# Early loading of the first MLP weights, and turnings without a tie to exponentials, in a two-layer decoder trunk

## The chip, the core and the metric

The kernel runs on one core of one Trainium2 chip. A core has a matrix engine (TensorE, called PE), a vector engine (VectorE, DVE), a scalar engine (ScalarE, ACT), a general engine (GpSimd, POOL) and a queue engine (SyncE, SP) that only issues DMA transfers here. Each engine works through its own list of instructions in order and waits on semaphores for the others. The metric is the device time of one execution in microseconds (us). The time before is 996.58 us, the median of three runs (995.73 to 997.40).

## What is computed

One sequence of 512 tokens of width 1024 goes through two layers, in float32. Layer A is latent attention with 8 heads (a compressed key and value of rank 256, a rotary part of 64), layer B is attention in a sliding window of 128 tokens with 16 query heads over 4 key heads, with a bias by distance and a sink for each head. Each mixer is followed by a LayerNorm and an MLP of width 4096, and the MLP by another LayerNorm:

```python
for l in range(2):
    if l == 0:
        y = _mla(x, ...)                      # softmax(q k') over c_kv, then w_uv, then o @ w_o
    else:
        k_band, v_band = _shared_kv(x, w_kv)  # bands of 2 * 128 tokens
        y = _swa(x, w_q, sinks, w_o, k_band, v_band, rel_bias)
    x = _layernorm(alpha * x + y, ln_mix_g[l], ln_mix_b[l])
    h = jax.nn.relu(x @ w_up[l])
    x = _layernorm(alpha * x + (h * h) @ w_down[l], ln_mlp_g[l], ln_mlp_b[l])
```

## The kernel before

**High and low parts.** A float32 product is made of three products of a shorter float type: every operand is split into a high part and the rest, and `three` (L106) gives the pairs high-high, high-low and low-high, which `group` (L103) sends to PE one after the other into one PSUM bank. `split` (L75) makes the parts: ACT copies the source into the short type (L77), and then DVE, in some cases POOL, subtracts the copy from the source (L81). So each weight tile takes a transfer, an ACT copy and a subtraction before PE can use it: the raw tile is `raw` or `wq`, the high part `wh`, the low part `wl`. The same function splits attention probabilities that have been turned (`pt`, in layer B `pth` and `ptl`) and heads' outputs (`oh`, `ol`).

**Order.** A scheduler orders the instructions on ACT, DVE and POOL by its own estimate of their times. The order of PE's instructions and of the SP transfers is that of the program text, through `pe` (L86). `behind` (L91) adds an edge: what is made inside is issued after the given instructions. `state["plain"]` holds the two instructions of the last split of an ordinary weight piece, `state["exp"]` the last exponential of layer B.

**The weight stream.** `queue` (L128) and `queue_seven` (L167) put weight pieces into the list `stream`, and `weights` (L314) prepares them four ahead of use, in the order of use. The raw tiles of ordinary pieces have two buffers, so a transfer waits until the subtraction of the piece two before has read its tile. The pieces of w_o are numbered 0 to 7 here. An MLP (width 4096 in four quarters) is computed with seven block products in place of eight, and `queue_seven` streams the blocks for one matrix and quarter. Its first pieces, `loaded` with block (0, 0) of the up matrix of quarter 0, fill a tile `wq` in two halves by two SP transfers of 512 KB (L210); their parts go into tiles set aside, w_fac and w_quada (`aside_of`, L157). `grown` ties those two splits behind the last ordinary split (L190), which is one of w_o.

**Layer A's attention** runs in `run_steps` (L542) over 32 units (h, i), head by query block of 128. Each unit computes scores (L1130) three units ahead of the turning (L1172), and a head's products with the values (`mix`, L1188) come two units behind. The scores end in a maximum on DVE (L1160), an exponential on ACT (L1165), a reciprocal (L1168) and a product (L1169) on DVE. Other work is put between the units from the list `fill`, whose entries have a cost, a unit by which they are due, a unit before which they don't come, and a function. The last entries load x's four token tiles (`load_x_tokens`, L925) and compute parts of the projection with w_o (`proj.part`). Then `proj.finish` (L501) makes the rest: the left halves of the four token tiles, then the right halves with, for each tile, the residual add (L584), the statistics, and `layer_norm` (L436, with its last steps at L446 and L449). The normed tile is turned on PE by eight transposes (L688) for the MLP.

**Layer B's attention** runs in the same way over 16 heads. `scores` (L1319) makes for one head the sums with the bias and the maxima (L1342), the negative maximum `nb` (L1346) and four exponentials (L1350) from two score banks. `turn` (L1362) transposes the probabilities in two halves (L1370, L1372) and splits each (`pth` on ACT, `ptl` on DVE). The first half is behind the last exponential, the one of the head two ahead (L1375). `mix` (L1385) multiplies by the values and adds two halves into `o` (L1402).

## Time and profile before

| What | us |
|---|---|
| median of three runs | 996.58 (995.73 to 997.40) |
| profiled execution | 997.49 |
| its span, first to last instruction | 995.7 |
| PE busy | 984.8 (99%) |
| DVE busy | 772.4 (78%) |
| ACT busy | 555.3 (56%) |
| POOL busy | 214.4 (22%) |

The granted clock of TensorE was 0.999 of full speed. Times in the text are counted from the start of the span. A row of the timeline has the start, the duration, the engine, the line, the operation with its output and input tiles and shapes, the number of instructions in the row and, in brackets, how long the engine had been idle before it and for whom it had waited. Matmuls overlap, so a matmul starts before the one ahead of it has ended. A row of the waits has the engine and line that waited, whom for, the us in total, the times and the longest. A row of the windows has the stretch, its length and each engine's busy time with its count of instructions, the granted clock, the busy share of the DMA engines and GB/s. A row of the DMA issues ends with the KB of one transfer and the us from issue to landing.

### The profile page before, as it was taken

How to read it: one execution, taken by the hardware profiler on the slowest of the kernel's cores; microseconds unless marked ns; L12 is line 12 of the kernel's file. 1: busy time of each engine (PE TensorE's matmuls, PEld its weight loads, DVE VectorE, ACT ScalarE, POOL GpSimd, SP SyncE). 2: the span in 40 equal slices, each digit the busy share in tenths (PEclk: the TensorE clock that was granted, in tenths of full speed). 3: DMA queues.
4: the chain of work that ended last, by engine and by line, in shares of the span. 5: the costliest groups of instructions: out<-in, count | busy, mean ns of one | idle time of the engine just before them, and what ended most of it. 6: DMA issues, size and time to landing. Idle time of an engine off the chain costs nothing.

```text
span 995.7 us, 15827 instructions
## 1 busy us (share of the span) xinstructions
PE 984.8 (99%) x6103; PEld 888.2 (89%) x6103; DVE 772.4 (78%) x1242; ACT 555.3 (56%) x850; POOL 214.4 (22%) x203
## 2 busy tenths in 40 slices
PE   9999999999999999999999999999999999999997
PEld 9888888998999999998898998889998999999986
DVE  6589857989778769786686778698985986898756
ACT  5556644467547547646145798546763663664620
POOL 1231001121212212210002775112131122023000
PEclk9999999999999999999999999999999999999999
DMA  7431227489889977964232212359798798798422
GB/s 261 142 90 43 68 103 226 103 184 226 152 183 238 171 170 218 224 109 145 67 106 96 86 65 75 110 144 211 181 203 183 176 207 175 167 261 143 115 95 85
DMA packets 60678, 149.55 MB, mean 150 GB/s; under 512 B 5259, under 2 KB 10300, under 8 KB 60604
## 3 DMA queue, kind: packets, MB, share of 16 engines
q0 software_dynamic: 24320, 58.73, 33.2%
q1 hardware_dynamic: 36140, 89.56, 27.0%
q8 instruction: 48, 0.79, 0.3%
q10 hardware_dynamic: 144, 0.26, 0.1%
q14 instruction: 26, 0.21, 0.1%
HBM read 146.41 MB, written 4.22 MB: 151 GB/s over the span
## 4 chain that ended last, share of the span: by engine, by line
PE 95%; DVE 2%; DMA 1%; ACT 1%; issue 0%; SPq 0%; DVEq 0%; POOL 0%; POOLq 0%
PE mm L105 87%; PE tr L105 5%; DMA wq<-in_up 1%; PE tr L1181 1%; PE tr L688 1%; PE tr L1370 1%; PE tr L1372 0%; ACT wh L77 0%; PE tr L461 0%; DVE mm L1342 0%; DVE x L446 0%; DVE wl L81 0%; DVE x L449 0%; PE tr L949 0%; DVE ptl L81 0%
## 5 line engine op out<-in xcount | busy, mean ns | idle before, releaser
L105 PE MATMUL mm<-wh,fac 128*128 128x512 f32 (+1 forms) x944 | 292.6, 386 | 0.0
L77 ACT ACTIVATE wh<-wq 128x1024 fp32r<-128x1024 f32 x164 | 173.8, 1061 | 185.0 <-PE mm L105 133.7
L81 DVE TENSOR_TENSOR wl<-wq,wh 128x1024 fp32r<-128x1024 f32 x164 | 199.4, 1220 | 68.1 <-ACT wh L77 66.6
L105 PE MATMUL mm<-xth,wh 128*128 128x256 f32 (+1 forms) x928 | 243.4, 290 | 0.0
L105 PE MATMUL mm<-xth,wl 128*128 128x256 f32 (+1 forms) x800 | 233.2, 292 | 0.0
L105 PEld LDWEIGHTS mm<-wh,fac 128*128 128x128 f32 x944 | 176.2, 188 | 35.6 <-DVE fac L81 0.6
L105 PE MATMUL mm<-xtl,wh 128*128 128x256 f32 (+1 forms) x672 | 197.1, 293 | 0.0
L105 PE MATMUL mm<-wl,fac 128*128 128x512 f32 (+1 forms) x472 | 182.3, 386 | 0.0
L105 PEld LDWEIGHTS mm<-xth,wh 128*128 128x128 f32 x928 | 168.6, 192 | 3.2
L105 PEld LDWEIGHTS mm<-xth,wl 128*128 128x128 f32 x800 | 153.2, 192 | 2.6
L77 ACT ACTIVATE wh<-raw 128x1024 fp32r<-128x1024 f32 (+3 forms) x86 | 85.1, 990 | 99.6 <-PE mm L105 56.9
L105 PEld LDWEIGHTS mm<-xtl,wh 128*128 128x128 f32 x672 | 128.7, 192 | 3.0
L201 POOL DMA_DIRECT2D wq<-in_up x64 | 77.5, 1237 | 202.0 <-DVE wl L81 192.1
L81 DVE TENSOR_TENSOR wl<-raw,wh 128x1024 fp32r<-128x1024 f32 (+2 forms) x66 | 77.0, 1173 | 35.8 <-ACT wh L77 35.5
L105 PEld LDWEIGHTS mm<-wl,fac 128*128 128x128 f32 x472 | 88.8, 188 | 16.5
L201 POOL DMA_DIRECT2D wq<-in_down x48 | 42.0, 875 | 187.2 <-DVE wl L81 181.3
L81 POOL TENSOR_TENSOR wl<-raw,wh 128x1024 fp32r<-128x1024 f32 (+2 forms) x20 | 41.3, 2067 | 87.5 <-ACT wh L77 82.0
L419 POOL TENSOR_TENSOR rs<-mv,half 128x1 f32<-128x1 f32 x16 | 8.8, 553 | 226.1 <-DVE mv L440 226.1
L105 PE MATMUL mm<-wh,oh 128*128 128x512 f32 x128 | 50.9, 398 | 0.0
L105 PE MATMUL mm<-wh,ol 128*128 128x512 f32 x128 | 50.1, 391 | 0.0
L105 PE MATMUL mm<-wl,oh 128*128 128x512 f32 x128 | 50.0, 390 | 0.0
L587 DVE TENSOR_TENSOR x<-mm,x 128x512 f32<-128x512 f32 (+1 forms) x49 | 32.9, 674 | 15.8 <-PE mm L105 15.7
(222 smaller groups left out, 1817.7 us busy)
## 6 DMA issues: line engine op xcount, KB each, us to landing
wq<-in_up POOLq DMA_DIRECT2D x64, 512.0 KB, 8.4
wq<-in_down POOLq DMA_DIRECT2D x48, 512.0 KB, 7.2
wq<-in_up SPq DMA_DIRECT2D x32, 512.0 KB, 6.8
raw<-in_down SPq DMA_DIRECT2D x28, 512.0 KB, 6.7
wq<-in_down SPq DMA_DIRECT2D x24, 512.0 KB, 5.9
raw<-in_up SPq DMA_DIRECT2D x16, 512.0 KB, 3.9
raw<-in_w_o SPq DMA_DIRECT2D x8, 512.0 KB, 5.1
raw<-in_w_sq SPq DMA_DIRECT2D x8, 512.0 KB, 3.3
```

The costliest lines, as they stand in the source:

```text
L77: high = nc.scalar.activation(dst_h, src, AF.Copy)
L81: low = (engine or nc.vector).tensor_sub(dst_l, src, f32(dst_h))
L105: pe(nc.tensor.matmul(dst, st, mv, start=first and i == 0, stop=last and i == len(pairs) - 1, **kw))
L201: nc.gpsimd.dma_start(half(a, jp), chunk(*more, jp), accum_op=ALU.add)
L419: state["rs"] = nc.gpsimd.tensor_tensor(r, v, half, ALU.pow)
L587: nc.vector.tensor_add(xs[t][:, c], b, xs[t][:, c])
L688: pe(nc.tensor.transpose(pt[:, a, :], xs[t][:, k * P : (k + 1) * P], ident))
L1181: pe(nc.tensor.transpose(pt[:, kb * P : (kb + 1) * P], p[:, kb * P : (kb + 1) * P], ident))
L1370: pe(nc.tensor.transpose(pt[:, a, 0:P], p[:, kb, P:256], ident))
```

## The change

The change has two parts.

In the first, the two SP transfers of layer A's first up block (the `wq` halves) become a function `preload`, which is put into `fill` right behind `load_x_tokens` and not before unit 17. So they are issued behind x's four tiles and ahead of w_o's piece 3, where before they came behind piece 7. `loaded` then issues no transfer for them, and `grown` no longer puts their splits behind the last ordinary split. Layer B's MLP calls no preload, and its code acts as before. On ACT and DVE the splits of w_fac and w_quada now stand ahead of those of w_o's pieces 4 and 5, behind the output of the last head; the split of piece 3 stands some places later than before, on ACT behind an exponential of head 7 and a turned block of head 6, on DVE behind a reciprocal, a small subtraction and a product.

In the second, `turn` of layer B ties the first half's split to `state["exp"]` only for heads 0 to 9. The order on the engines changes for the splits of heads 11 and 12 only: head 11's first half now stands ahead of its second half and of head 13's exponentials, and head 12's two halves stand ahead of head 14's exponentials. The sum `o` of head 10 now stands ahead of head 14's `nb`. The orders on PE and POOL are the same as before.

```diff
-        stream, off_ring, later = [], [], []
+        stream, off_ring, later, preloads = [], [], [], {}
...
+            early = set()
+
             def grown(a, jp, *more, aside=None):
                 wh, wl = tiles_of_weights(aside)
                 after = None
-                if aside:
+                if aside and not early:
                     after = state.pop("plain", None)
...
+            def preload():
+                for jp in range(2):
+                    early.add(jp)
+                    pe(nc.sync.dma_start(half("a", jp), chunk(0, 0, jp)))
+
+            preloads.setdefault((name, key), preload)
+
             def loaded(a, jp, at, *more, aside=None):
-                pe(nc.sync.dma_start(half(a, jp), chunk(*at, jp)))
+                if a == "b" or jp not in early:
+                    pe(nc.sync.dma_start(half(a, jp), chunk(*at, jp)))
                 return grown(a, jp, *more, aside=aside)
...
             fill.append((0, 99, -9, load_x_tokens))
+            fill.append((0, 99, 17, preloads["up", "U"]))
             for t in range(2):
                 for kp in range(3):
                     fill.append((1.3, 99, max(8 * kp + 10, 29 * t), lambda t=t, kp=kp: proj.part(t, kp)))
...
-                        with behind((state["exp"],)):
+                        with behind((state["exp"],) if h < 10 else None):
                             split(pth[:, 0:2, :], ptl[:, 0:2, :], pt)
```

## The prediction

> **What bounds the kernel now.** I read the busy times first, then the chain that ended last, then the waits of TensorE (PE), and last a table of PE's busy time in four stretches.

> ```profile
> span 995.7 us, 15827 instructions
> PE 984.8 (99%) x6103; PEld 888.2 (89%) x6103; DVE 772.4 (78%) x1242; ACT 555.3 (56%) x850; POOL 214.4 (22%) x203
> ...
> PE 95%; DVE 2%; DMA 1%; ACT 1%; issue 0%; SPq 0%; DVEq 0%; POOL 0%; POOLq 0%
> ...
> PE tr L1370 <- DVE ptl L81: 1.7, 3, 0.9
> ...
> PE tr L688 <- DVE x L449: 0.4, 1, 0.4
> ...
> 0.00:173.00 173.00, 171.11 (x921) 148.85 (x922) 128.11 (x348) 94.28 (x204) 27.86 (x29) 1.00 0.40 133
> 173.00:605.00 432.00, 432.00 (x2776) 393.55 (x2775) 338.19 (x512) 252.97 (x389) 108.97 (x98) 1.00 0.63 150
> 605.00:625.00 20.00, 18.28 (x120) 15.89 (x119) 15.21 (x52) 16.96 (x53) 9.67 (x11) 1.00 0.09 28
> 625.00:995.70 370.70, 363.39 (x2291) 329.93 (x2289) 290.87 (x332) 191.10 (x207) 67.93 (x67) 1.00 0.70 165
> ```

> PE is busy for 984.8 of 995.7 us and is 95% of the chain, at a granted clock of 1.00 in all four stretches. So a change gains only where PE waits, and loses only where it makes PE wait. The table places the 10.9 us without work: 1.9 before 173 us, none from 173 to 605, 1.7 between 605 and 625 (layer B's last heads) and 7.3 behind 625, which is the last LayerNorm after PE's end. The two parts of the change touch 123 to 173 us and 605 to 625 us. Of the idle time there they can remove the 0.4 us at line 688 and the three waits at line 1370, 1.7 us together: some 2.1 us by idle time, and no other gain exists in this profile. PE's own instructions and their order are the same in both programs; so are GpSimd's (POOL). VectorE (DVE), ScalarE (ACT) and the DMA queue of SyncE (SP) change their order.

> **Part 1: the first MLP weights behind x's tokens.** It adds and removes no instruction. Two SP transfers of 512 KB (`wq`, line 210) go from behind the last w_o piece to ahead of w_o piece 3, and so past pieces 3 to 7; their two splits (tiles w_fac and w_quada) go ahead of the splits of w_o pieces 4 and 5 on ACT and DVE.

> The gain first. The wait at line 688 is for the LayerNorm of the first token tile:

> ```profile
> 170.88 0.39 PE L105 MATMUL mm<-wh,ol 128*128 128x512 f32 x1
> 171.71 1.09 PE L688 MATMUL tr<-ident,x 128*128 128x128 f32 x8 [0.44 <-DVE x L449]
> ...
> 164.94 1.22 DVE L81 TENSOR_TENSOR w_fac<-wq,w_fac 128x1024 fp32r<-128x1024 f32 x1
> ...
> 170.37 1.28 DVE L449 SCALAR_TENSOR_TENSOR x<-x,rs,gb 128x1024 f32<-128x1024 f32 x1
> ```

> Matmuls of this group start 0.23 us apart (133.72 to 133.95, quoted below). The transposes started 0.83 behind the matmul before them, 0.60 late. Before, the DVE subtractions of w_fac and w_quada (from 164.94, the second in one piece behind it) stood directly ahead of the first tile's residual add and LayerNorm; afterwards they are done some 12 us earlier, so the wait should go: -0.60, of which 0.44 shows as idle.

> The price. Piece 3 of w_o is what the two transfers are put ahead of, and it is already late:

> ```profile
> 124.18 8.62 SPq L142 DMA_DIRECT2D raw<-in_w_o  x3
> ...
> raw<-in_w_o SPq DMA_DIRECT2D x1, 512.0 KB, 5.9
> ...
> 126.00:130.00 4.00, 4.00 (x21) 3.28 (x20) 3.73 (x16) 2.22 (x6) 0.00 (x0) 1.00 0.99 396
> ...
> 130.13 1.06 ACT L77 ACTIVATE wh<-raw 128x1024 fp32r<-128x1024 f32 x1 [0.82 <-DMA raw<-in_w_o]
> ```

> The first of the three issues is piece 3: issued at 124.18, landed 5.9 us later at 130.08, and ACT, which had waited 0.82 us for it, begins its split at 130.13. In the 4 us before, the DMA engines are 99% busy at 396 GB/s, with x's four tiles ahead of the piece. So two more transfers in front add their full time: 524,288 bytes at 396 GB/s are 1.32 us each, 2.65 together, and the ACT copy moves to about 132.75. [...]

> What is queued behind that copy and its DVE subtraction:

> ```profile
> 131.23 1.23 DVE L81 TENSOR_TENSOR wl<-raw,wh 128x1024 fp32r<-128x1024 f32 x1 [0.90 <-ACT wh L77]
> 132.37 0.16 DVE L1168 RECIPROCAL ri<-sm 128x1 f32<-128x1 f32 x1
> ...
> 133.22 0.43 DVE L1160 CUSTOM_DVE_ANT_0 mm<-mm,const 128x256 f32<-128x256 f32 x1 [0.18 <-PE mm L105]
> 133.57 0.14 DVE L1160 DVE_READ_ACCUMULATOR2_ANT mx<- 128x1 f32 x1
> ...
> 133.72 0.40 PE L105 MATMUL mm<-wh,oh 128*128 128x512 f32 x1
> 133.95 0.40 PE L105 MATMUL mm<-wl,oh 128*128 128x512 f32 x1
> 134.31 0.50 PE L105 MATMUL mm<-wh,ol 128*128 128x512 f32 x1
> ```

> In the changed order ACT does an exponential and a turned block first and then waits with the copy; DVE does the reciprocal, one small subtraction and one product first, then the subtraction of piece 3, then the maximum of line 1160 and then the low half `ol` of head 5's output. Before, `ol` started at 133.57 (with the accumulator read) and PE's matmul on it at 134.31, 0.74 later; that one started 0.36 behind its predecessor, so PE already waited 0.13 there and has no slack. Afterwards: copy at 132.75; subtraction 1.10 later (131.23 less 130.13) at 133.85; next instruction 1.14 later (132.37 less 131.23), the maximum at 134.99; `ol` 0.35 later (133.57 less 133.22) at 135.34; PE's matmul at 136.08. That is 1.77 later than 134.31, on PE's path. Everything that hangs on PE then moves by 1.77 with it; DVE and ACT have room from 137 to 150 (heads 6 and 7, few splits), so I find no second stall there.

> PE then works through until the transposes: they come at 171.71 - 0.60 + 1.77 = 172.88. The LayerNorm's last step ended at 170.37 + 1.28 = 171.65; its residual add now waits for PE rather than for the two subtractions, so it ends near 172.2, ahead of 172.88. Part 1 costs 172.88 - 171.71 = **+1.17 us**. Bounds: if the piece came no later (the transfers share the engines and its own finish first), only the gain stays, -0.60. The pair of transfers has also been seen landing slower:

> ```profile
> 162.44 1.06 ACT L77 ACTIVATE w_fac<-wq 128x1024 fp32r<-128x1024 f32 x1 [0.47 <-DMA wq<-in_up]
> ...
> 164.11 1.06 ACT L77 ACTIVATE w_quada<-wq 128x1024 fp32r<-128x1024 f32 x1 [0.60 <-DMA wq<-in_up]
> ```

> Both copies waited for the DMA, 1.67 us apart; at that spacing the pair takes 3.34 and part 1 costs 0.69 more, +1.86. I take 1.32, since the 4 us of 396 GB/s are the very stretch where the transfers will run.

> The second consumer is the last w_o piece, number 7. Its transfer needs the tile that the subtraction of piece 5 frees, and that now stands behind w_fac and w_quada:

> ```profile
> 150.08 0.69 DVE L81 TENSOR_TENSOR ol<-mm,oh 128x512 fp32r<-128x512 f32 x1 [3.94 <-ACT oh L77]
> 152.01 2.54 DVE L81 TENSOR_TENSOR wl<-raw,wh 128x1024 fp32r<-128x1024 f32 x2 [1.25 <-ACT wh L77]
> ...
> 153.27 1.64 SPq L142 DMA_DIRECT2D raw<-in_w_o  x2
> ...
> raw<-in_w_o SPq DMA_DIRECT2D x1, 512.0 KB, 6.2
> ...
> raw<-in_up SPq DMA_DIRECT2D x1, 512.0 KB, 7.8
> ...
> 164.50 0.40 PE L105 MATMUL mm<-wl,oh 128*128 128x512 f32 x1
> ```

> Before, the subtractions of pieces 4 and 5 run from 152.01 to 154.55, and transfers 6 and 7 follow them (issued from 153.27 on; the 6.2 us is piece 7's). Afterwards `ol` comes at 150.08 + 1.77 = 151.85; w_fac at about 152.85 behind its ACT copy; w_quada 1.14 later; pieces 4 and 5 from 155.1 to 157.5. Piece 7 is issued near 157.5, lands 6.2 later at 163.7, is copied (1.10) and subtracted (1.23) by about 166.1. PE first needs it at 164.50 + 1.77 = 166.27. I cost this at nothing, with 0.2 us of cover; what it costs without the cover is a rival below.

> **Part 2: the turnings of layer B's heads 10 to 15.** The tie to the last exponential is dropped. Only heads 11 and 12 change place on ACT and DVE; the others stand where they stood. One of the three waits at line 1370 is this:

> ```profile
> 615.57 0.33 PE L1370 MATMUL tr<-ident,p 128*128 128x128 f32 x1 [0.65 <-DVE ptl L81]
> 617.82 0.40 PE L105 MATMUL mm<-wh,oh 128*128 128x512 f32 x1
> ...
> 612.29 0.56 DVE L81 TENSOR_TENSOR ptl<-tr,pth 128x384 fp32r<-128x384 f32 x1
> 614.63 0.22 DVE L1346 TENSOR_SCALAR nb<-mm,sink 128x4 f32<-128x4 f32 x1
> 614.86 0.66 DVE L81 TENSOR_TENSOR ptl<-tr,pth 128x512 fp32r<-128x512 f32 x1
> 615.45 0.68 DVE L1402 TENSOR_TENSOR o<-mm,low 64x512 f32<-64x512 f32 x1
> ...
> 615.37 0.37 ACT L1350 ACTIVATE p<-mm,nb 128x128 f32<-128x128 f32 x1
> 616.09 0.20 ACT L1350 ACTIVATION_READ_ACCUMULATOR p<-mm,nb 128x1 f32 x1
> ```

> PE waits 0.65 us idle (about 0.8 in issue order) for the subtraction at 614.86, head 11's first half, which stood behind head 13's exponentials. In the new order it stands at 612.29, ahead of the second half, so this wait goes: -0.8. The other two waits hang on head 10's split, whose place is the same; they stay. What is late next: the maxima of head 14 behind 612.29 move back by 0.59 (615.45 less 614.86), and the sum `o`, about 0.6, now stands ahead of head 14's `nb`: that comes at 614.63 + 0.59 + 0.1 + 0.6 = 615.9 instead of 614.63, the exponential near 616.2 instead of 615.37. The w_so matmul at 617.82 takes the score bank that head 14's second exponential frees; that one ended at 616.09 + 0.20, 0.92 behind the first one's start, so the bank is free near 617.1 to 617.2, while PE would come at 617.82 - 0.8 = 617.0. A new wait of about 0.2: part 2 brings **-0.6 us**, between 0 (the new wait eats it all) and -1.7 (all three waits go).

> **The sum.** +1.17 - 0.6 = about +0.6 us. The profiled execution took 997.49, its span and 1.79 around it; it would become 998.1. The median of the three runs is 996.58, so the forecast is 997.2. A change of this kernel under 0.2%, 2.0 us, can't be told from none (its three runs alone span 1.7 us), so this counts as the same.

> **The rivals.**
> Slower: piece 7 of w_o lands too late. Three rows above bear on it: the issue moves 2.9 us back, the cover is 0.2 us, and a later SP transfer of the same size in this stretch took 7.8 us. At 7.8 it lands at 165.3, its subtraction is done near 167.7, and PE waits 1.4 on top: +2.0, 998.6; each further 0.1 us adds as much. It decides from a landing of 7.8 us on. Against it: the two transfers that followed piece 7 and shared the engines with it are gone by then, though gb's take their place.
> Faster: piece 3 isn't delayed and the waits at line 1370 all go: -0.60 - 1.7 = -2.3, 994.3. For it only the sizes of the idle times speak; against it the 99% busy DMA engines and head 10's unchanged order. With piece 3 undelayed and part 2 as forecast it is -1.2, 995.4, which counts as the same.
> No effect: piece 3 is delayed by just the 0.6 that the wait at 688 gives back, and the new wait in layer B eats the gain there: 996.6. For it speaks that both gains end in another wait; against it 1.32 us per transfer.

> **How the numbers follow.** My forecast with its neighbours inside 0.2% (+1.86 instead of +1.17 for part 1, no effect, -1.2): 0.70. The late piece 7, or it with the slower pair of transfers: 0.21. The faster case: 0.09. So faster 0.09, same 0.70, slower 0.21. The range takes in -1.2 with 0.3 of run scatter below (995.1) and piece 7 at 8.4 us above (+2.6, 999.2). The likeliest case's own range is 996.4 to 998.2.

> **What would show it.** In the new profile: ACT's copy of piece 3 near 132.75 with a longer DMA wait; a PE wait of 1.5 to 1.9 us near 134 to 136 for `ol`; no wait at line 688; w_fac and w_quada split near 152 to 155; piece 7's copy near 164 and whether a PE wait for `wl` follows near 166; one wait fewer at line 1370 and a small one of a w_so matmul for an exponential near 617. The prediction is wrong if piece 3 lands before 131.4, if PE stalls over 1 us for piece 7, or if w_fac's early split waits for memory that the attention still holds and blocks ACT.

## The result, and the profile after

| | before | changed |
|---|---|---|
| median of 22 executions each (us) | 997.08 (995.53 to 998.02) | 998.98 (996.75 to 1002.51) |
| profiled execution (us) | 997.49 | 996.75 |
| its span (us) | 995.7 | 994.9 |

The ratio is 1.0026, with a 95% interval of 1.0016 to 1.0035: the change makes the kernel about 0.26% slower, by 1.9 us of median. The forecast was 997.2 and no difference that can be measured. The spread is the first thing to see. The unchanged kernel's executions lie within 2.5 us of each other, the changed one's within 5.8, and the profiled one is the fastest of them.

The page of the changed kernel (busy times and the chain) and its table of PE's waits:

```profile
span 994.9 us, 15824 instructions
PE 983.4 (99%) x6103; PEld 887.4 (89%) x6103; DVE 772.5 (78%) x1242; ACT 555.0 (56%) x850; POOL 215.4 (22%) x203
```

```profile
PE tr L1381 <- DVE ptl L81: 1.1, 2, 0.9
...
PE mm L105 <- DVE nb L1174: 1.0, 1, 1.0
...
PE mm L105 <- ACT oh L77: 0.4, 1, 0.4
```

(The lines of the changed kernel stand some 10 lines further down: 688 is now 698, 1370 is 1381.) The wait at the turning in layer A is gone, one of the three waits of layer B is gone, and two waits for head 5's output are new. The first of them is for the high part `oh`, which ACT now makes behind its copy of piece 3; the second is for the low part `ol`, and the view puts it down to `nb`, the instruction behind `ol` on DVE. The prediction had one wait, for `ol`. Their places, in the timeline of PE in the changed kernel:

```profile
132.54 0.39 PE L105 MATMUL mm<-wh,ol 128*128 128x512 f32 x1
133.33 0.50 PE L105 MATMUL mm<-wh,oh 128*128 128x512 f32 x1 [0.40 <-ACT oh L77]
...
135.05 0.50 PE L105 MATMUL mm<-wh,ol 128*128 128x512 f32 x1 [0.99 <-DVE nb L1174]
...
171.80 1.03 PE L698 MATMUL tr<-ident,x 128*128 128x128 f32 x8
...
609.80 0.30 PE L1381 MATMUL tr<-ident,p 128*128 128x128 f32 x1 [0.89 <-DVE ptl L81]
...
617.27 0.39 PE L105 MATMUL mm<-wl,oh 128*128 128x512 f32 x1
```

and the same matmuls in the kernel before, where the prediction doesn't show them:

```profile
133.49 0.39 PE L105 MATMUL mm<-wh,ol 128*128 128x512 f32 x1
...
609.90 0.30 PE L1370 MATMUL tr<-ident,p 128*128 128x128 f32 x1 [0.89 <-DVE ptl L81]
...
618.06 0.40 PE L105 MATMUL mm<-wl,oh 128*128 128x512 f32 x1
```

PE's order is the same in both programs, so the distance between the same matmuls of two traces shows what each stretch gained or lost. Ahead of the waits the changed execution is 0.95 us early (132.54 against 133.49), 0.80 of which it has gained by 7 us already, at the start of the program, which differs by that much from one execution to the next. Behind the two waits it is 0.74 late (135.05 against 134.31): the waits cost 1.69. At the turning it is 0.09 late (171.80 against 171.71): the wait that went gave back 0.65. At the first turning of layer B that waits it is 0.10 early, and behind the second 0.79 early (617.27 against 618.06): part 2 gave 0.69. The sum of the three is +0.35 us in this execution.

So this trace confirms nearly every term of the prediction, and doesn't show the loss. The other executions do. Each has a mean granted clock: the slower ones have a lower one. Of the changed kernel's executions, these 22 and 5 later ones, 13 have a clock of 0.998 or 0.999 and take 997.9 us on average; 14 have 0.994 to 0.997 and take 1001.1.

### The profile page after: what moved, and what is told of

It reads as the page before. It is cut to its first block, busy times and chain, and to the rows that moved or that the text cites. A ratio compares the mean times of both kernels' runs of the same rounds, so it can differ in the third digit from the quotient of the medians.

```text
span 994.9 us, 15824 instructions
## 1 busy us (share of the span) xinstructions
PE 983.4 (99%) x6103; PEld 887.4 (89%) x6103; DVE 772.5 (78%) x1242; ACT 555.0 (56%) x850; POOL 215.4 (22%) x203
## 4 chain that ended last, share of the span: by engine, by line
PE 96%; DVE 1%; DMA 1%; ACT 1%; issue 0%; SPq 0%; DVEq 0%; ACTq 0%
PE mm L105 88%; PE tr L105 5%; DMA raw<-in_w_o 1%; PE tr L698 1%; PE tr L1191 1%; PE tr L1381 1%; PE tr L1383 0%; ACT wh L77 0%; DMA xraw<-in_xT 0%; PE tr L471 0%; DVE wl L81 0%; PE tr L959 0%; PE mm L1099 0%; DVE mm L1353 0%; DVE ql L81 0%
## 5 line engine op out<-in xcount | busy, mean ns | idle before, releaser
L105 PE MATMUL mm<-wh,fac 128*128 128x512 f32 (+1 forms) x944 | 292.6, 386 | 0.0
L77 ACT ACTIVATE wh<-wq 128x1024 fp32r<-128x1024 f32 x164 | 173.7, 1060 | 185.0 <-PE mm L105 133.3
L81 DVE TENSOR_TENSOR wl<-wq,wh 128x1024 fp32r<-128x1024 f32 x164 | 199.6, 1221 | 67.4 <-ACT wh L77 66.5
L105 PE MATMUL mm<-xth,wh 128*128 128x256 f32 (+1 forms) x928 | 243.4, 290 | 0.0
L105 PE MATMUL mm<-xth,wl 128*128 128x256 f32 (+1 forms) x800 | 233.2, 292 | 0.0
L105 PEld LDWEIGHTS mm<-wh,fac 128*128 128x128 f32 x944 | 176.3, 188 | 35.6 <-DVE fac L81 0.6
L105 PE MATMUL mm<-xtl,wh 128*128 128x256 f32 (+1 forms) x672 | 197.1, 293 | 0.0
L105 PE MATMUL mm<-wl,fac 128*128 128x512 f32 (+1 forms) x472 | 182.3, 386 | 0.0
L105 PEld LDWEIGHTS mm<-xth,wh 128*128 128x128 f32 x928 | 168.6, 192 | 3.2
L105 PEld LDWEIGHTS mm<-xth,wl 128*128 128x128 f32 x800 | 153.2, 192 | 2.6
L77 ACT ACTIVATE wh<-raw 128x1024 fp32r<-128x1024 f32 (+3 forms) x86 | 85.0, 990 | 96.7 <-PE mm L105 54.7
L105 PEld LDWEIGHTS mm<-xtl,wh 128*128 128x128 f32 x672 | 128.7, 192 | 3.0
L81 DVE TENSOR_TENSOR wl<-raw,wh 128x1024 fp32r<-128x1024 f32 (+2 forms) x66 | 77.0, 1174 | 34.3 <-ACT wh L77 34.1
L105 PEld LDWEIGHTS mm<-wl,fac 128*128 128x128 f32 x472 | 88.8, 188 | 16.5
L81 POOL TENSOR_TENSOR wl<-raw,wh 128x1024 fp32r<-128x1024 f32 (+2 forms) x20 | 41.2, 2064 | 87.2 <-ACT wh L77 79.3
L105 PE MATMUL mm<-wh,oh 128*128 128x512 f32 x128 | 51.0, 399 | 0.4 <-ACT oh L77 0.4
L105 PE MATMUL mm<-wh,ol 128*128 128x512 f32 x128 | 50.1, 392 | 1.0 <-DVE nb L1174 1.0
L105 PE MATMUL mm<-wl,oh 128*128 128x512 f32 x128 | 49.9, 390 | 0.0
## 6 DMA issues: line engine op xcount, KB each, us to landing
wq<-in_up POOLq DMA_DIRECT2D x64, 512.0 KB, 8.2
wq<-in_down POOLq DMA_DIRECT2D x48, 512.0 KB, 7.2
wq<-in_up SPq DMA_DIRECT2D x32, 512.0 KB, 6.4
raw<-in_down SPq DMA_DIRECT2D x28, 512.0 KB, 6.3
wq<-in_down SPq DMA_DIRECT2D x24, 512.0 KB, 5.3
raw<-in_up SPq DMA_DIRECT2D x16, 512.0 KB, 4.3
raw<-in_w_o SPq DMA_DIRECT2D x8, 512.0 KB, 3.3
raw<-in_w_sq SPq DMA_DIRECT2D x8, 512.0 KB, 3.2
```

The costliest lines, as they stand in the source:

```text
L77: high = nc.scalar.activation(dst_h, src, AF.Copy)
L81: low = (engine or nc.vector).tensor_sub(dst_l, src, f32(dst_h))
L105: pe(nc.tensor.matmul(dst, st, mv, start=first and i == 0, stop=last and i == len(pairs) - 1, **kw))
```

## The experiments

**Part 1 and part 2 apart.** Part 1 alone undoes the edit in `turn`:

```diff
-                        with behind((state["exp"],) if h < 10 else None):
+                        with behind((state["exp"],)):
```

> Part 1 alone; layer B's turnings keep their ties. The profiled execution of the changed kernel is no slower than before, but 10 of its 22 executions took 1000.5 to 1002.5 us, at a mean granted clock of 0.994 to 0.997, where the others had 0.998 or 0.999. Theory C (clock): part 1's PE wait of 1.4 us near 133 us makes the granted clock fall for some microseconds in some executions. Then about 4 in 10 executions of this kernel are 3 to 5 us longer than the rest at a clock of 0.994 to 0.997; its shorter ones lie near 998 (997.1 + 1.0), its median between 998 and 1001. Theory B (part 2 brings the long executions): none here; all within 996.5 to 999 at 0.998 or 0.999. Theory L (a transfer lands later in some executions and PE only waits longer): long ones here too, but with the full clock outside the wait.

Measured: 1000.50 us median against 996.46, ratio 1.0042 (1.0028 to 1.0056); executions at 998.03, 999.60, 1000.50, 1001.53 and 1001.77, with clocks of 0.998, 0.998, 0.996, 0.994 and 0.994. Part 2 alone leaves everything else as it was before:

> Part 2 alone; the first MLP weights are loaded where they were before. Theory C: no long executions, since layer B loses a PE wait and gains only a small one; 0.6 to 0.7 us faster than before, near 996.4, all at a clock of 0.998 or 0.999. Theory B: long executions here, about 4 in 10 above 1000. Theory L: as theory C.

Measured: 996.44 us against 996.46, ratio 0.9997 (0.9988 to 1.0006), all clocks from 0.997 to 0.999, none longer than 997.30. The median doesn't show the gain of 0.7 us, but 0.9993 lies well within the interval, and the trace of this kernel has the wait at line 1370 twice (1.1 us) in place of three times. So the long executions and the loss belong to part 1; theory B falls.

**The clock, seen directly.** The changed kernel and part 1 alone were run again for further profiles.

> The changed kernel once more, to have a second profile of it and more executions with their clocks. Theory C: 3 to 5 in 10 executions above 1000 at a clock of 0.994 to 0.997; if the profiled one is among them, its table of stretches shows a clock under 1.00 in the microseconds behind 133 us and nowhere else before the end.

> Part 1 alone once more, for the same reason. Theory C: 4 to 6 in 10 executions are 3 to 4 us longer at a clock of 0.994 to 0.997; in a profile of one of these the clock falls behind 133 us and the wait itself is as long as in the others (1.7 to 2.0 us). Theory L: the wait is 3 us longer.

Measured: the changed kernel 999.37 us against 996.56, ratio 1.0031 (1.0017 to 1.0044), four of five executions at 0.995 or 0.996; part 1 alone 1000.50, ratio 1.0038 (1.0023 to 1.0053), three of four at 0.994 to 0.997. Both profiled executions were among those. PE's busy time, the granted clock and the DMA load of the changed kernel, in three stretches of 3.41 us:

```profile
133.11:136.52 3.41, 1.64 (x7) 0.71 (x7) 2.23 (x5) 1.59 (x4) 0.00 (x0) 1.00 0.17 34
136.53:139.94 3.41, 3.41 (x15) 3.22 (x14) 1.86 (x6) 0.96 (x4) 0.00 (x0) 0.50 0.34 131
139.94:143.35 3.41, 3.41 (x17) 2.77 (x16) 2.50 (x9) 1.90 (x6) 0.00 (x0) 1.00 0.00 0
```

The clock is 1.00 in the stretch with the waits, 0.50 in the next one and 1.00 again; the rows for the other stretches up to 980 us show 1.00. PE is busy throughout the middle stretch but gets through about half as much: against the unchanged kernel it falls from 1.76 us late behind the waits to 3.33, so it loses 1.57 us of 3.41. In the profile of part 1 alone:

```profile
133.43:136.84 3.41, 0.99 (x4) 0.30 (x2) 2.15 (x5) 1.54 (x2) 0.00 (x0) 1.00 0.06 22
136.85:140.25 3.40, 3.33 (x12) 3.05 (x13) 1.40 (x6) 1.06 (x3) 0.00 (x0) 0.50 0.47 154
```

The stretches are not chosen freely. In the first profiles of both kernels the clock is full in one piece of 986.452 us (from 6.90 to 993.35 us before, from 3.83 to 990.28 in the changed kernel), which is 289 times 3.413; it is half for 3.41 and 3.40 us in the rows above and for 6.82 in two rows further down. So I laid stretches of 3.413 us out from the moments at which the clock changed, called windows from here on, and counted PE's idle time in them. The clock fell after windows with 1.77 us of idle time (1.64 busy, above), 2.42 and, further down, 2.59, and stayed at half after one with 2.95. It did not fall after the window with the most idle time ahead of PE's end in the kernel before (1.07, the first row) or in the first profile of part 1 alone (1.45, the second):

```profile
607.65:611.06 3.41, 2.34 (x14) 1.56 (x13) 3.31 (x14) 2.75 (x8) 1.71 (x2) 1.00 0.48 154
```

```profile
132.00:135.41 3.41, 1.96 (x10) 1.05 (x8) 2.03 (x4) 1.54 (x2) 0.00 (x0) 1.00 0.13 48
```

The window in which PE's work ends is a case of its own. In the second profile of part 1 alone it has 1.77 us of idle time too, and the next one, without any work on PE, is still at the full clock:

```profile
990.18:993.59 3.41, 1.65 (x14) 1.44 (x13) 2.43 (x6) 0.00 (x0) 0.46 (x1) 1.00 0.37 154
993.59:997.00 3.41, 0.00 (x0) 0.00 (x0) 2.34 (x4) 0.00 (x0) 0.08 (x1) 1.00 0.26 95
```

From the first rise of the clock to PE's end, in the whole first profiles of both kernels and in the rows shown from the others, no window with 1.55 us or less (that one is at PE's end in the kernel before) was followed by half the clock, and every one with 2.42 or more was; of the two at 1.77 one was. Whether the idle time alone decides is not shown; if it does, and at the same amount everywhere, my estimate from these windows is near 1.77 us. Theory C holds. Theory L holds for a part as well: piece 3 was under way longer in these executions, and PE is 2.07 and 2.80 us later behind the waits than ahead of them, against 1.69 and 1.94 in the first profiles of the two kernels. PE's two waits, in this profile of the changed kernel:

```profile
PE mm L105 <- DVE nb L1174: 1.0, 1, 1.0
PE mm L105 <- ACT oh L77: 0.8, 1, 0.8
```

and in this one of part 1 alone:

```profile
PE mm L105 <- ACT oh L77: 1.5, 1, 1.5
...
PE mm L105 <- DVE nb L1174: 1.0, 1, 1.0
```

In the first profile of the changed kernel the one for `oh` was 0.4. So a longer wait for the transfer goes ahead of the fall, and the clock adds to it.

**The wait filled.** The stall stays, but PE is given work in it:

```diff
+                    if self.name == "w_o" and (t, k) == (0, 5) and self.b.get(t) is b:
+                        nil = [(zeros, zeros[:, None, :].broadcast_to([P, 4, P]))]
+                        b4 = b.rearrange("p (a b) -> p a b", a=4)
+                        group(b4, nil * 2, False, False)
+                        group(b, pairs[:2], False, False)
+                        group(b4, nil * 4, False, False)
+                        group(b, pairs[2:], False, False)
+                        continue
```

> Part 1 alone, with six matmuls of zeros by zeros added to PE's order inside the stall of part 1: two ahead of the first matmul that waits there and four ahead of the second. They add zeros to the running sum and need nothing, so PE works through most of the wait. Theory C: piece 3 is as late as in part 1 alone and the shorter executions take about the same (998, up to 0.3 more), but the long ones with the lower clock are gone. Theory L: the long executions stay, since the transfers are the same.

Measured: 998.83 us against 996.46, ratio 1.0020 (1.0011 to 1.0030); ten executions from 997.67 to 999.77, all clocks from 0.997 to 0.999. In the profile piece 3 is as late as without the filling, PE is 1.77 us later behind the place than ahead of it, and it is busy all the while:

```profile
132.18:135.59 3.41, 3.39 (x16) 2.21 (x15) 2.17 (x5) 1.55 (x2) 0.00 (x0) 1.00 0.13 48
```

Six matmuls that compute nothing make the median 1.7 us lower than part 1 alone (1000.50). That is so although PE waits 0.5 us at 518 us in this profile and in the next kernel's, for a split behind layer A's last LayerNorm (`xtl`), and in no other; why is open. With only the two ahead of the first waiting matmul:

> Part 1 alone with only the two matmuls of zeros ahead of the first waiting matmul; the second wait of about 1.0 us stays. Theory C, if what counts is the idle time within a few microseconds: about 1.0 to 1.2 us of idle is what the unchanged kernel has near 610 us (0.89 and 0.18) without a fall, so the long executions are gone as with six; near 998.8. If any wait of 1 us there is enough, they stay.

Measured: 998.54 us against 996.56, ratio 1.0021 (1.0012 to 1.0031); nine of ten executions at 0.998 or 0.999, one at 0.996 (1001.24). Its profile (1000.37 us) happens to have the longest waits of all with these transfers, 1.68 and 0.98 us, and no fall; this execution is long by its waits, at the full clock. In the grid of this trace a boundary falls between the two waits, and the windows have 1.26 and 1.41 us of idle time, less than the 1.77 ahead of the fall in the changed kernel:

```profile
131.70:135.12 3.42, 2.16 (x14) 1.59 (x12) 0.09 (x1) 1.17 (x2) 0.00 (x0) 1.00 0.47 185
135.12:138.53 3.41, 2.00 (x10) 1.50 (x11) 2.66 (x7) 1.34 (x4) 0.00 (x0) 1.00 0.31 105
```

**The wait doubled.**

```diff
+                idle = dr.tile([2, P, 2, 512], F32, name="idle")
+                for jp in range(2):
+                    pe(nc.sync.dma_start(idle[jp], chunk(0, 0, jp)))
                 for jp in range(2):
                     early.add(jp)
...
+                with behind(state["third"] if h == 5 else None):
                     split(oh[h // 4][:, h % 4, :], ol[h // 4][:, h % 4, :], b)
```

Here `state["third"]` holds the two instructions of piece 3's split.

> Part 1 alone, with two more transfers of 512 KB (copies into memory that nothing reads) ahead of the two early ones, and head 5's output tied behind piece 3's split, so that it keeps waiting for it. Piece 3 lands some 2.6 us later again and PE's wait near 133 us grows from about 1.8 to about 4.4 us. By the wait alone: some 2.6 us over the shorter executions of part 1 alone, near 1000.7. Theory C: the granted clock now falls in nearly every execution, its mean is 0.996 or less, the time is 3 us longer still, near 1004, and the profile shows where the clock fell. Theory L: near 1000.7 at the full clock.

Measured: 1004.22 us against 996.56, ratio 1.0076 (1.0061 to 1.0091), four executions from 1003.38 to 1004.86, all at 0.995 or 0.996. PE waited longer than expected, 5.6 us in one piece and 0.2, and the clock was half for two windows:

```profile
132.74:136.15 3.41, 0.82 (x5) 0.34 (x3) 1.16 (x5) 0.56 (x2) 0.00 (x0) 1.00 0.97 369
136.16:139.57 3.41, 0.46 (x1) 0.46 (x2) 0.96 (x1) 1.54 (x2) 0.00 (x0) 0.50 0.09 37
139.57:142.98 3.41, 3.25 (x10) 2.36 (x10) 1.36 (x3) 0.49 (x1) 0.00 (x0) 0.50 0.48 154
142.99:146.39 3.40, 3.40 (x19) 2.81 (x19) 2.77 (x11) 1.73 (x5) 0.00 (x0) 1.00 0.00 0
```

No execution has more than 0.996, and the time no longer scatters (1.5 us). PE was busy for only 0.46 and 3.25 us of the two windows at half the clock, so by an estimate from these rows (half of the busy time) they cost 1.9 us, where two filled ones would cost 3.4. The match of 1004 is thus partly luck: more wait and less clock than expected.

**Why the transfers vary.** The early weights are stored so that a row of one transfer is 2 KB; x's and w_o's rows have 4 KB. The same number of bytes was taken from w_o, in place of the MLP block, whose own weights this kernel doesn't load:

```diff
-                    pe(nc.sync.dma_start(half("a", jp), chunk(0, 0, jp)))
+                    pe(nc.sync.dma_start(flat(half("a", jp)), io["w_o"][6 + jp]))
```

> Part 1 alone, but the two early transfers take 512 KB each from w_o's pieces 6 and 7, whose rows of 4 KB lie together, in place of the MLP weights, whose rows here are 2 KB (so the MLP of layer A computes with wrong weights in one block). In the five profiles with the early MLP weights ahead of piece 3, PE's two waits near 133 us took 1.7 to 3.5 us in all, by how long piece 3 was under way. If the 2 KB rows make the transfers slow and uneven: piece 3 now lands as the rows of w_o and x did before, 1.3 us per transfer, PE's waits are 1.7 to 1.8 us in the profile, and the executions lie within 997.3 to 999 with few at a clock under 0.998. If any transfer there varies so: times from 998 to 1002 as in part 1 alone, half of them at 0.994 to 0.997.

Measured: 997.66 us against 996.58, ratio 1.0012 (1.0002 to 1.0021); ten of eleven executions from 996.83 to 998.95, one at 1001.12 (clock 0.997). DMA load from 126 to 130 us, share and GB/s last, in this kernel, in the changed one, and in the half filled one:

```profile
126.00:128.00 2.00, 2.00 (x13) 1.64 (x12) 1.73 (x8) 1.51 (x5) 0.00 (x0) 1.00 0.99 377
128.00:130.00 2.00, 2.00 (x11) 1.61 (x10) 1.38 (x9) 0.84 (x4) 0.00 (x0) 1.00 1.04 420
```

```profile
126.00:128.00 2.00, 2.00 (x13) 1.66 (x12) 1.83 (x7) 1.26 (x4) 0.00 (x0) 1.00 0.88 291
128.00:130.00 2.00, 2.00 (x11) 1.62 (x11) 1.33 (x8) 0.89 (x6) 0.00 (x0) 1.00 1.06 408
```

```profile
126.00:128.00 2.00, 2.00 (x12) 1.57 (x10) 1.93 (x9) 1.00 (x4) 0.00 (x0) 1.00 0.73 253
128.00:130.00 2.00, 2.00 (x14) 1.69 (x12) 1.66 (x8) 0.90 (x4) 0.00 (x0) 1.00 0.86 308
```

With the rows of 4 KB PE is 1.48 us later behind the waits than ahead of them, less than the 1.7 to 1.8 expected; with the MLP weights' rows it was 1.69 to 3.45 in six profiles. The three executions start these transfers at different times (in the changed one x's last two tiles are issued from 122.13 us on, in the half filled one from 122.58), but the order is the same in both rows: 377, 291 and 253 GB/s, then 420, 408 and 308. So the slow and uneven transfers go with the MLP weights as their source, and so do the waits that are long enough for the clock to fall. The two sources differ in the length of the rows and also in where they lie in memory; which of the two it is wasn't separated, and the one side rests on one profile and eleven executions.

**The transfers behind piece 3.** The same early loading, one entry later:

```diff
-            fill.append((0, 99, 17, preloads["up", "U"]))
             for t in range(2):
                 for kp in range(3):
                     fill.append((1.3, 99, max(8 * kp + 10, 29 * t), lambda t=t, kp=kp: proj.part(t, kp)))
+                    if t == kp == 0:
+                        fill.append((0, 99, 17, preloads["up", "U"]))
```

> Both parts, but the two early transfers are issued behind piece 3 of w_o instead of ahead of it, so piece 3 lands when it did before; the early splits and layer B's part stay. Theory C: no wait near 133 us, so no long executions, the wait at line 688 is gone (-0.6) and layer B's too (-0.7): about 1.2 us faster than before, near 995.9. If the long executions come from the early splits (piece 7 of w_o late, theory L), they are still here, with a PE wait for wl near 165 us.

> The version with the early transfers behind piece 3 once more, beside the unchanged kernel on the same chip, to narrow its interval: by the sum of its two gains (0.65 at line 688 and 0.68 in layer B) 1.3 us faster than before, ratio 0.9987, no execution at a clock under 0.997.

Measured: 995.31 us against 996.46, ratio 0.9990 (0.9981 to 0.9999), and again 995.62 against 996.58, ratio 0.9986 (0.9977 to 0.9995), no execution at a clock under 0.997. (One further execution of the first run took 3390.93 us at the full clock; no trace of it exists, and its cause is open.) It beats both kernels, the one before by about 1 us; the two gains alone would be 1.3. PE's waits in its first profile, all of them:

```profile
PE tr L1382 <- DVE ptl L81: 1.1, 2, 0.9
PE mm L105 <- POOL zeros L360: 1.0, 1, 1.0
PE mm L105 <- DVE ql L81: 0.5, 2, 0.2
```

## Why the prediction was wrong

The mechanism of every step in the sum was right, and each size but one was close; the median left the forecast by 1.8 us through that one and through an effect that wasn't in the sum.

- The wait at line 688 goes: forecast -0.60, measured -0.63 to -0.69 in the profiles with part 1.
- Part 2: forecast -0.6 with a new wait of about 0.2 near 617 us; measured -0.68 to -0.70 in five profiles. The new wait is there: from the last score matmul (616.74) to the second w_so matmul (617.27) it takes 0.53 us in the changed kernel and 0.35 (617.71 to 618.06) in the one before, 0.18 more. The old wait was 0.87, a little more than the 0.8 of the sum.
- The late piece 7 of w_o, the rival on the slow side, didn't happen. In the changed kernel ACT and DVE take it so:

```profile
161.31 1.06 ACT L77 ACTIVATE wh<-raw 128x1024 fp32r<-128x1024 f32 x1 [1.55 <-DMA raw<-in_w_o]
```

```profile
162.79 1.21 DVE L81 TENSOR_TENSOR wl<-raw,wh 128x1024 fp32r<-128x1024 f32 x1
```

It is done at 164.00, over 1 us ahead of need (164.50 and the 0.7 that PE is late there): its transfer took 4.8 us from issue to landing, where the sum had the 6.2 of the kernel before. Theory L's form of it (a wait for `wl` near 165) falls in all profiles.
- The price of part 1, +1.77 us by two transfers of 1.32 us: measured 1.48 with rows of 4 KB, 1.69 to 3.45 (six profiles; 1.77 in the one with the wait filled) with the rows that the change really moves. The step that failed is "I take 1.32, since the 4 us of 396 GB/s are the very stretch where the transfers will run". The stretch was the same, the transfers were not: those 396 GB/s were measured on x and w_o. The row for the right ones stood in the prediction, 1.67 us apart, and was used only as a bound; by it the wait would be 1.77 + 0.69 = 2.46 us. As the average of the six, 2.3, the wait costs half a microsecond more.
- The term that was missing: what PE's wait does to its clock. The argument that a change "loses only where it makes PE wait" priced a wait at its length. Behind the windows with 1.77 and 2.42 us of idle time, in the two profiles with a fall, the next window cost 1.57 and 1.54 us more. The forecast wait, 1.77 late and by my estimate some 1.4 of it idle (1.39 of 1.69 in the first profile), lay under both; the real ones left 0.98 to 2.42 us of idle time in the window with most of it, by the transfers' luck and by where the grid lies. With a mean clock of 0.996 or less as its mark, the fall happened in 17 of 36 executions with part 1's order and the MLP weights, in 1 of 20 with the wait filled wholly or half, and in none of 61 of the unchanged kernel. The mark misses some: the second profile of part 1 alone shows a fall at a mean of 0.997. The executions of the changed kernel without it average 997.9, 0.8 over before, near the forecast's +0.6; those with it 1001.1.
- The range's top, 999.2, holds the median, but 10 of the 22 executions lie above it; the chance of 0.21 for slower was given to the wrong mechanism.

Open stays what makes single transfers of the MLP weights slow in some executions and not in others. Open also stays whether some executions lose more than one window: by an estimate from the traces, one window of 3.41 us at half the clock lowers the mean over 998 us by 0.0017, and four of the 36 executions are at 0.994. None of these was profiled.

## What to carry to other kernels

When PE is the bound, price a new wait twice: its length, and what the granted clock does after it. Here 1.77 and 2.42 us of idle time within 3.41 came ahead of half the clock, and that cost 1.57 and 1.54 us more. Spread over two windows (1.26 and 1.41 us idle), or filled with matmuls that add zeros (0.02 and 0.05), the wait cost only its length here. Take a transfer's duration from rows of the same tensor and not from the bandwidth of another one at the same place. And when a profile looks faster than the median, look at the spread and the clocks of all executions before explaining anything by that profile.
